# Delta-net layer: a pair's scales on VectorE, longer waits in the key chain, the last gate group ahead of the values, the gate sums with the decays

## The chip, the cores and the metric

The kernel runs on one core of a Trainium2 chip. The metric is the time of one execution on the device in microseconds; the runs shown are three of the kernel before. A profile of one execution shows what TensorE (PE, with its weight loads PEld), VectorE (DVE), ScalarE (ACT), GpSimd (POOL) and the DMA queue of SyncE (SP) did.

## The reference

The program is a two-layer trunk over 256 tokens of 1024 features in float32. Each layer has three parts, each between two RMS norms and added to the running state h: a SwiGLU block, a mixer, and a second SwiGLU block. Layer 0's mixer is a gated short convolution. Layer 1's mixer, the one that the change touches, is a gated delta-net:

- a projection gives queries and keys (8 heads of 128 features), values and output gates z (16 heads of 128), and two small columns per value head, b and a;
- q, k and v pass a causal convolution of width 4 and a silu; q and k are normalized to unit length;
- beta = sigmoid(b), and g = -exp(a_log) softplus(a + dt_bias) is a log decay per token and head;
- per head a state S follows S_t = a_t S_{t-1} (I - b_t k_t k_t^T) + b_t k_t v_t^T, o_t = S_t^T q_t, in chunked form: within a chunk a lower triangular matrix of decayed, beta-scaled key products is inverted;
- o is RMS-normalized, multiplied by silu(z), and projected back to 1024 features.

## The kernel before

Tokens are two tiles of 128 (t = 0, 1). Every float32 product is made from three TensorE products: a weight is split into a rounded part hi (ScalarE copy, L111) and the rest lo (VectorE subtraction, L113), and so is the activation. A weight unit is 128 x 1024: its DMA goes into one of 3 raw buffers, and hi and lo take one of 8 buffers each. Seven parts follow one another on PE: SwiGLU, mixer and SwiGLU of each layer, with an out-projection after each; in all but the delta-net they are dense matmuls with little between them.

The delta-net part (`gdn_proj`, about 668 to 930 us of the span) is a main line of dense matmuls, between which chains of small dependent steps are laid:

- The main line: the head slabs (b, a and the first seven key and query tiles, with the activation stationary), then nine more key and query tiles (`stat_group`, L248 to L250, weights stationary, 24 matmuls of 256 columns a tile), then the gate groups z 0, 1, 2 (`z_group`: `act_group`, L216 to L220, 48 matmuls of 512 columns a group, and a silu into a gate tile), then the value groups 0 to 3 (`v_group`, 96 matmuls of 256 columns each), then z group 3, then the out-projection (`out_proj`, L293 to L295, six matmuls a step).
- The ticker: after every 6 matmuls of `act_group`, every 12 of `stat_group` and every step of the out-projection, `tk.tick()` lets each chain advance to its next `yield`. `yield n` means: go on n ticks later. So the ticks set in what place of the program a chain's instructions stand. A planner then orders each engine's queue when the program is built: it takes that place as the priority and may put an instruction earlier when, by its own estimate, those ahead of it are not ready.
- `gates()` (L472) turns b and a into beta and the log decays g, and sums g over tokens by two small matmuls (L498, L499) with two exponentials behind them (L500, L501: `etail`, `eg`). It runs when the first head slab of t = 1 is done. `decays()` (L503) builds for four groups of four heads the products `gu` (L512), waits for the first convolved key (`while not convs`), and makes the decay matrices (L520 matmul, L522 exponential, L523 mask on GpSimd).
- `kq_raw` convolves a key or query tile (L548 on ScalarE, three steps L550 on VectorE) and takes its silu (L537).
- `kq_chain` (L569) goes through the 8 key heads in 4 pairs. A head waits until KQ_WAIT = 3 ticks after its silu; then come four transposes (L582), the key products (L585), and on ScalarE the copies and sums of squares (L594). Then the pair's scales: epsilon added to the sums (L598, GpSimd), reciprocal (L600, VectorE), times beta (L603, twice, GpSimd). VectorE scales and masks the products (L609, 8 instructions) and ScalarE copies the 32x32 diagonal blocks out (L616, 8). GpSimd makes three more small values (L618 a power, L620, L622). `yield 1` ends a pair. All heads and pairs take their PSUM from the same four banks.
- `invert()` (L631) starts when the chain has ended: VectorE transposes the blocks and inverts them in 62 dependent steps (L641, L643), and INV_WAIT = 37 ticks after its start the matmuls that build the full inverses begin (L671 to L703).
- `v_pair` convolves a pair of value tiles, and V_WAIT = 4 ticks later transposes them (L721). `scan(gi)` waits for its values and its inverse, then goes through solve (L735), intra-chunk product (L744), state (L775, L784) for t = 0, then solve and product for t = 1. `z_chain(gi, t)` waits for the scan's output scale, multiplies it into the gate tile (L810), transposes (L815) and splits it (L818, L819) into the operand of the out-projection.
- The out-projection takes its operands through `view.get`, which ticks on by itself until the one it wants exists. While `tail[0]` is false, the chains' PSUM banks (`side_bank`) come from the pool that the out-projection accumulates in; afterwards from the main line's pool.

Gate tiles, values, solutions and scan outputs share 22 slab slots; the scaled products take 8 larger ones.

Of the kernel before, what the change touches and what calls it, by code (L numbers as in the profile page):

```python
# [21 lines left out]
NG = 4  # L22
B32 = 32
EPS = 1e-6
# [6 lines left out]
NSMALL = 22  # L31
NBIG = 8
NROW = 3
KQ_WAIT = 3
INV_WAIT = 37
V_WAIT = 4
SCAN_WAIT = 2
# [13 lines left out]
def trunk_kernel(ctx: ExitStack, tc: tile.TileContext, x, norm_g, w_gu, w_dn, sc_in, sc_cw, sc_out,  # L51
# [389 lines left out]
    def gdn_proj(xh, xl, mid):  # L441
# [25 lines left out]
        def side_bank():  # L467
            return (ps if tail[0] else ps_acc).tile([P, 4, P], F32, name="mm" if tail[0] else "acc")
# [3 lines left out]
        def gates():  # L472
            def sm(name):
                return sp.tile([P, NT, NVH], F32, name=name, bufs=1)

            a, u, e, z, q = sm("ga"), sm("gb"), sm("gc"), sm("gd"), sm("ge")
            G.tensor_tensor(a, ba[:, :, NVH:], bc(dtb, NT), ALU.add)
            G.tensor_scalar(u, a, 0.0, -2.0, ALU.max, ALU.mult)
            G.tensor_tensor(e, a, u, ALU.add)
            S.activation(e, e, AF.Exp)  # L480
            S.activation(al, al, AF.Exp)
            S.activation(beta, ba[:, :, 0:NVH], AF.Exp, scale=-1.0)

            V.tensor_scalar(z, e, 2.0, None, ALU.add)
            V.reciprocal(z, z)
            V.tensor_tensor(z, z, e, ALU.mult)
            V.tensor_tensor(u, z, z, ALU.mult)
            V.tensor_scalar(q, u, 1.0 / 19.0, None, ALU.mult)
            for k in (17, 15, 13, 11, 9, 7, 5, 3):
                V.scalar_tensor_tensor(q, q, 1.0 / k, u, ALU.add, ALU.mult)  # L490
            V.scalar_tensor_tensor(q, q, 1.0, z, ALU.add, ALU.mult)
            V.tensor_scalar(a, a, 0.0, None, ALU.max)
            V.scalar_tensor_tensor(q, q, 2.0, a, ALU.mult, ALU.add)
            V.scalar_tensor_tensor(g, q, -1.0, bc(al, NT), ALU.mult, ALU.mult)
            G.tensor_scalar(beta, beta, 1.0, None, ALU.add)
            V.reciprocal(beta, beta)
            pg = side_bank().rearrange("p a b -> p (a b)")[:, 0:2 * NVH].rearrange("p (t n) -> p t n", t=NT)
            PE.matmul(pg[:, 0, :], lhsT=tri_s, rhs=g[:, 0, :], start=True, stop=True)  # L498
            PE.matmul(pg[:, 1, :], lhsT=tri_u, rhs=g[:, 1, :], start=True, stop=True)  # L499
            S.activation(etail, pg[:, 0, :], AF.Exp)  # L500
            S.activation(eg, pg[:, 1, :], AF.Exp)  # L501

        def decays():  # L503
            gus = []
            for gi in range(NG):
                gu = big([P, NT, 4, P], F32, "gu")
                for t in range(NT):
                    if 2 * gi + t < GUACT:
                        for hv in range(4):
                            S.activation(gu[:, t, hv, :], tri_u, AF.Copy, scale=g[:, t, 4 * gi + hv:4 * gi + hv + 1])  # L510
                        continue
                    V.tensor_tensor(gu[:, t], bc(tri_u, 4),  # L512
                                    g[:, t, 4 * gi:4 * gi + 4].unsqueeze(2).broadcast_to([P, 4, P]), ALU.mult)
                gus.append(gu)
            while not convs:
                yield 1
            for gi in range(NG):
                for t in range(NT):
                    pd = side_bank()
                    PE.matmul(pd, lhsT=tri_s, rhs=gus[gi][:, t], start=True, stop=True)  # L520
                    d = slab([P, 4, P], F32, "dec")
                    last_exp[0] = S.activation(d, pd, AF.Exp).ins  # L522
                    G.affine_select(d, d, pattern=[[0, 4], [1, P]], compare_op=ALU.is_ge, fill=0.0, base=0,  # L523
                                    channel_multiplier=-1)
                    dec[t][gi] = d
                if gi % 2:
                    yield 1
            dec_done[0] = True
            while convs:
                kq_silu(*convs.pop(0))  # L530
# [38 lines left out]
        def kq_chain():  # L569

            for gi in range(NG):
                ss = sp.tile([P, NT, 2, 2], F32, name="kss", bufs=2)
                k1 = slab([P, 2, 2, P], F32, "kq1")
                pkq = []
                for i in range(2):
                    kh = 2 * gi + i
                    while kq[kh] is None or tk.now < kq_time[kh] + KQ_WAIT:
                        yield 1
                    tp = side_bank().rearrange("p (t c) d -> p t c d", t=NT)
                    for t in range(NT):  # L580
                        for c in range(2):
                            PE.transpose(tp[:, t, c, :], kq[kh][:, c, t * P:(t + 1) * P], ident)  # L582
                    pk = side_bank().rearrange("p (t c) d -> p t c d", t=NT)
                    for t in range(NT):
                        PE.matmul(pk[:, t, :, :], lhsT=kq[kh][:, 0, t * P:(t + 1) * P],  # L585
                                  rhs=kq[kh][:, :, t * P:(t + 1) * P], start=True, stop=True)
                    pkq.append(pk)
                    S.activation(ktok[:, kh, :], tp[:, 0, 0, :], AF.Copy)
                    S.activation(k1[:, i, :, :], kq[kh][:, :, P:], AF.Copy)
                    kq1[kh] = k1[:, i, :, :]  # L590
                    for t in range(NT):
                        for c in range(2):
                            junk = sp.tile([P, 512], mybir.dt.bfloat16, name="junk", bufs=1)
                            S.activation(junk[:, 0:P], tp[:, t, c, :], AF.Square, accum_out=ss[:, t, c, i:i + 1])  # L594
                    yield 1
                while dec[1][gi] is None:
                    yield 1
                G.tensor_scalar(ss, ss, EPS, None, ALU.add)  # L598
                rk = sp.tile([P, NT, 2], F32, name="rk", bufs=2)
                V.reciprocal(rk, ss[:, :, 0, :])  # L600
                dd = small(f"dsc{gi}", 8).rearrange("p (t n) -> p t n", t=NT)
                for t in range(NT):
                    G.tensor_tensor(dd[:, t, :].rearrange("p (k v) -> p k v", k=2),  # L603
                                    beta[:, t, 4 * gi:4 * gi + 4].rearrange("p (k v) -> p k v", k=2),
                                    rk[:, t, :].unsqueeze(2).broadcast_to([P, 2, 2]), ALU.mult)
                for t in range(NT):
                    m = big([P, 4, 2, P], F32, "KQ")
                    for hv in range(4):
                        V.scalar_tensor_tensor(m[:, hv, :, :], pkq[hv // 2][:, t, :, :], dd[:, t, hv:hv + 1],  # L609
                                               bc(dec[t][gi][:, hv, :], 2), ALU.mult, ALU.mult)  # L610
                    KQ[gi][t] = m
                    for b in range(4):
                        r = slice(b * B32, (b + 1) * B32)
                        o = Ld[r, :, 8 * gi + t:8 * gi + t + 7:2].rearrange("p i v -> p v i")
                        i_ = m[r, :, 0, b * B32:(b + 1) * B32]
                        S.activation(o, i_, AF.Copy)  # L616
                n = small(f"nk{gi}", 4).rearrange("p (t n) -> p t n", t=NT)
                G.tensor_tensor(n, ss[:, :, 0, :], phalf.rearrange("p (t n) -> p t n", t=NT), ALU.pow)  # L618
                q = small(f"eq{gi}", 4).rearrange("p (t n) -> p t n", t=NT)
                G.tensor_scalar(q, ss[:, :, 1, :], 128.0 * EPS, None, ALU.mult)  # L620
                w = small(f"wt{gi}", 4)
                G.tensor_tensor(w, etail[:, 4 * gi:4 * gi + 4], dd[:, 0, :], ALU.mult)  # L622
                Dsc[gi], nk[gi], eq[gi], wt[gi] = dd, n, q, w
                yield 1
            tk.start(invert())


# [194 lines left out]
        def z_group(gi):  # L822
            w = load_slab(gdn_z[gi])
            for t in range(NT):
                pt = ps.tile([P, 512], F32, name="mm")
                act_group(pt, w, t, xh, xl)
                zs = slab([P, 4, P], F32, "zs")
                silu(zs, pt.rearrange("p (h d) -> p h d", h=4))
                tk.start(z_chain(gi, t, zs))
# [48 lines left out]
                    stat_group(pt[:, j, :], w, (2 * i + j) * P, xh, xl)  # L878
                tk.start(v_pair(gi, i, pt, tiles))

        for gi in range(NG - 1):
            z_group(gi)
        for gi in range(NG):
            v_group(gi)
        z_group(NG - 1)
        tail[0] = True

        def view(hs):
# [115 lines left out]
```

## Time and profile before

| | |
|---|---|
| runs | 1131.45, 1131.49, 1133.35 us; median 1131.49 |
| profiled execution | 1134.7 us, of which the span from first to last instruction 1132.9 |
| mean granted TensorE clock | 0.994 |
| busy | PE 1096.3 us (97%), PEld 941.8 (83%), DVE 748.1 (66%), ACT 652.3 (58%), POOL 88.7 (8%) |
| share of the chain that ended last | PE 75%, DVE 8%, ACT 6%, DMA 5%, issue 3%, POOL 2% |

PE's busy time is modelled for matmuls that overlap, so 97% busy is not the peak rate; but idle time on PE is real. A wait of an engine is shown with what released it. The granted clock is 1.00 at 2.4 GHz and 0.50 at 1.2 GHz.

### The profile page before, as it was taken

How to read it: one execution, taken by the hardware profiler on the slowest of the kernel's cores; microseconds unless marked ns; L12 is line 12 of the kernel's file. 1: busy time of each engine (PE TensorE's matmuls, PEld its weight loads, DVE VectorE, ACT ScalarE, POOL GpSimd, SP SyncE). 2: the span in 40 equal slices, each digit the busy share in tenths (PEclk: the TensorE clock that was granted, in tenths of full speed). 3: DMA queues.
4: the chain of work that ended last, by engine and by line, in shares of the span. 5: the costliest groups of instructions: out<-in, count | busy, mean ns of one | idle time of the engine just before them, and what ended most of it. 6: DMA issues, size and time to landing. Idle time of an engine off the chain costs nothing.

```text
span 1132.9 us, 16811 instructions
## 1 busy us (share of the span) xinstructions
PE 1096.3 (97%) x6272; PEld 941.8 (83%) x6272; DVE 748.1 (66%) x1137; ACT 652.3 (58%) x1203; POOL 88.7 (8%) x165
## 2 busy tenths in 40 slices
PE   6999999999999999999999999889899999999997
PEld 5888887788788888788888877868899887888886
DVE  5677735687777673577765478768956657767543
ACT  5665634545556663556664458784587645666432
POOL 2000000000110000010000012110051212000000
PEclk9999999999999999999999999999899999999999
DMA  7766555666565555577554653237342354665552
GB/s 255 236 195 207 176 177 176 207 186 199 186 209 196 194 186 170 165 225 214 184 195 167 189 185 115 85 102 223 113 132 76 120 165 173 213 204 181 191 167 75
DMA packets 55953, 198.64 MB, mean 175 GB/s; under 512 B 6720, under 2 KB 7232, under 8 KB 55872
## 3 DMA queue, kind: packets, MB, share of 16 engines
q1 hardware_dynamic: 55872, 197.58, 53.8%
q8 instruction: 49, 0.80, 0.3%
q14 instruction: 32, 0.26, 0.1%
HBM read 196.51 MB, written 1.05 MB: 174 GB/s over the span
## 4 chain that ended last, share of the span: by engine, by line
PE 75%; DVE 8%; ACT 6%; DMA 5%; issue 3%; POOL 2%; SPq 0%; DVEq 0%; POOLq 0%; ACTq 0%
PE mm L268 24%; PE mm L271 12%; PE acc L294 7%; PE acc L295 7%; PE acc L293 7%; PE mm L216 3%; PE mm L217 3%; PE mm L220 3%; DVE wlo L113 3%; DMA raw<-in_sc_in 2%; ACT whi L111 2%; ACT blk L616 1%; DVE kq L550 1%; ACT junk L145 1%; PE mm L171 1%
## 5 line engine op out<-in xcount | busy, mean ns | idle before, releaser
L113 DVE TENSOR_TENSOR wlo<-raw,whi 128x1024 fp32r<-128x1024 f32 (+2 forms) x362 | 437.9, 1220 | 243.0 <-ACT whi L111 208.3
L111 ACT ACTIVATE whi<-raw 128x1024 fp32r<-128x1024 f32 (+2 forms) x362 | 376.4, 1052 | 234.7 <-PE acc L295 104.2
L268 PE MATMUL mm<-x,whi 128*128 128x512 f32 x1312 | 329.4, 393 | 0.0
L268 PEld LDWEIGHTS mm<-x,whi 128*128 128x128 f32 x1312 | 235.9, 189 | 42.2
L271 PEld LDWEIGHTS mm<-x,wlo 128*128 128x128 f32 x1312 | 179.0, 190 | 12.8
L271 PE MATMUL mm<-x,wlo 128*128 128x256 f32 x1312 | 182.9, 282 | 0.0
L293 PE MATMUL acc<-whi,hb 128*128 128x512 f32 x352 | 136.6, 388 | 0.7 <-ACT hb L437 0.7
L294 PE MATMUL acc<-wlo,hb 128*128 128x512 f32 x352 | 135.7, 385 | 0.3 <-DVE wlo L113 0.3
L295 PE MATMUL acc<-whi,hb 128*128 128x512 f32 x352 | 135.5, 385 | 0.0
L217 PE MATMUL mm<-wlo,x 128*128 128x512 f32 (+1 forms) x240 | 95.0, 396 | 1.9 <-DVE wlo L113 1.9
L216 PE MATMUL mm<-whi,x 128*128 128x512 f32 (+1 forms) x240 | 95.4, 398 | 0.8 <-ACT x L173 0.7
L278 ACT ACTIVATE corr<-mm 128x256 f32<-128x256 f32 x164 | 60.6, 375 | 60.4 <-PE mm L271 59.9
L220 PE MATMUL mm<-whi,x 128*128 128x512 f32 (+1 forms) x240 | 88.8, 392 | 0.0
L293 PEld LDWEIGHTS acc<-whi,hb 128*128 128x128 f32 x352 | 66.2, 188 | 14.1 <-ACT hb L437 1.1
L294 PEld LDWEIGHTS acc<-wlo,hb 128*128 128x128 f32 x352 | 66.2, 188 | 13.8 <-DVE wlo L113 0.8
L295 PEld LDWEIGHTS acc<-whi,hb 128*128 128x128 f32 x352 | 66.1, 188 | 13.6 <-DVE hb L438 0.4
L151 POOL TENSOR_SCALAR rstd<-ss 128x1 f32<-128x1 f32 x24 | 12.2, 509 | 821.1 <-ACT junk L145 821.1
L248 PE MATMUL mm<-x,whi 128*128 128x256 f32 x200 | 60.3, 302 | 2.0 <-DVE kq L550 2.0
L249 PE MATMUL mm<-x,whi 128*128 128x256 f32 x200 | 59.0, 295 | 0.0
L250 PE MATMUL mm<-x,wlo 128*128 128x256 f32 x200 | 58.5, 292 | 0.0
L217 PEld LDWEIGHTS mm<-wlo,x 128*128 128x128 f32 x240 | 45.7, 191 | 12.4 <-DVE wlo L113 4.0
L216 PEld LDWEIGHTS mm<-whi,x 128*128 128x128 f32 x240 | 45.7, 191 | 10.9 <-ACT x L173 2.4
(208 smaller groups left out, 1231.1 us busy)
## 6 DMA issues: line engine op xcount, KB each, us to landing
raw<-in_w_gu SPq DMA_DIRECT2D x176, 512.0 KB, 4.1
raw<-in_w_dn SPq DMA_DIRECT2D x88, 512.0 KB, 3.6
raw<-in_sc_in SPq DMA_DIRECT2D x24, 512.0 KB, 4.0
raw<-in_gdn_z SPq DMA_DIRECT2D x16, 512.0 KB, 3.8
raw<-in_gdn_v SPq DMA_DIRECT2D x16, 512.0 KB, 4.2
raw<-in_gdn_out SPq DMA_DIRECT2D x16, 512.0 KB, 3.7
gamma<-in_norm_g SPq DMA_DIRECT2D x12, 512.0 KB, 5.6
raw<-in_gdn_a SPq DMA_DIRECT2D x9, 512.0 KB, 4.2
```

What stands on the lines that cost most here:

```text
L111: S.activation(hi[:, r], raw[:, r], AF.Copy)
L113: V.tensor_tensor(lo[:, r], raw[:, r], hi[:, r], ALU.subtract)
L216: PE.matmul(pt, lhsT=xh[:, t, k, :], rhs=hi, start=(k == 0), stop=False)
L217: PE.matmul(pt, lhsT=xh[:, t, k, :], rhs=lo, start=False, stop=False)
L220: PE.matmul(pt, lhsT=xl[:, t, j, :], rhs=part(j)[0], start=False, stop=(j == KD - 1))
L248: PE.matmul(ptile, lhsT=hi, rhs=h2, start=(k == 0), stop=False)
L268: PE.matmul(flat, lhsT=part(k, 0), rhs=xx[:, k].rearrange("p h t q -> p (h t q)"), start=(k == 0), stop=False)
L271: PE.matmul(flat[:, T:], lhsT=part(k, 1), rhs=xx[:, k, 0].rearrange("p t q -> p (t q)"), start=False, stop=(k == KD - 1))
L278: S.activation(c, pt[:, 1, :], AF.Copy)
L293: PE.matmul(o, lhsT=yh(c, t), rhs=hi[:, r], start=(c == 0), stop=False)
L294: PE.matmul(o, lhsT=yh(c, t), rhs=lo[:, r], start=False, stop=False)
L295: i = PE.matmul(o, lhsT=yl(c, t), rhs=hi[:, r], start=False, stop=(c == n - 1)).ins
```

## The change

Four edits, all in `gdn_proj`:

1. The epsilon add and the two products with beta of each pair move from GpSimd to VectorE.
2. KQ_WAIT becomes 5, and a pair of the key chain ends with `yield PAIR_WAIT` (3) where it was `yield 1`.
3. All four z groups come ahead of the value groups; before, the fourth came behind them.
4. The sums of the log decays, with their exponentials, leave `gates()` for a function of their own, `gate_sums()`, which `decays()` calls when the first convolved key is there.

```diff
@@ -31,7 +31,8 @@
 NSMALL = 22
 NBIG = 8
 NROW = 3
-KQ_WAIT = 3
+KQ_WAIT = 5
+PAIR_WAIT = 3
 INV_WAIT = 37
 V_WAIT = 4
 SCAN_WAIT = 2
@@ -494,6 +495,8 @@
             V.scalar_tensor_tensor(g, q, -1.0, bc(al, NT), ALU.mult, ALU.mult)
             G.tensor_scalar(beta, beta, 1.0, None, ALU.add)
             V.reciprocal(beta, beta)
+
+        def gate_sums():
             pg = side_bank().rearrange("p a b -> p (a b)")[:, 0:2 * NVH].rearrange("p (t n) -> p t n", t=NT)
             PE.matmul(pg[:, 0, :], lhsT=tri_s, rhs=g[:, 0, :], start=True, stop=True)
             PE.matmul(pg[:, 1, :], lhsT=tri_u, rhs=g[:, 1, :], start=True, stop=True)
@@ -514,6 +517,7 @@
                 gus.append(gu)
             while not convs:
                 yield 1
+            gate_sums()
             for gi in range(NG):
                 for t in range(NT):
                     pd = side_bank()
@@ -595,12 +599,12 @@
                     yield 1
                 while dec[1][gi] is None:
                     yield 1
-                G.tensor_scalar(ss, ss, EPS, None, ALU.add)
+                V.tensor_scalar(ss, ss, EPS, None, ALU.add)
                 rk = sp.tile([P, NT, 2], F32, name="rk", bufs=2)
                 V.reciprocal(rk, ss[:, :, 0, :])
                 dd = small(f"dsc{gi}", 8).rearrange("p (t n) -> p t n", t=NT)
                 for t in range(NT):
-                    G.tensor_tensor(dd[:, t, :].rearrange("p (k v) -> p k v", k=2),
+                    V.tensor_tensor(dd[:, t, :].rearrange("p (k v) -> p k v", k=2),
                                     beta[:, t, 4 * gi:4 * gi + 4].rearrange("p (k v) -> p k v", k=2),
                                     rk[:, t, :].unsqueeze(2).broadcast_to([P, 2, 2]), ALU.mult)
                 for t in range(NT):
@@ -621,7 +625,7 @@
                 w = small(f"wt{gi}", 4)
                 G.tensor_tensor(w, etail[:, 4 * gi:4 * gi + 4], dd[:, 0, :], ALU.mult)
                 Dsc[gi], nk[gi], eq[gi], wt[gi] = dd, n, q, w
-                yield 1
+                yield PAIR_WAIT
             tk.start(invert())
 
 
@@ -878,11 +882,10 @@
                     stat_group(pt[:, j, :], w, (2 * i + j) * P, xh, xl)
                 tk.start(v_pair(gi, i, pt, tiles))
 
-        for gi in range(NG - 1):
+        for gi in range(NG):
             z_group(gi)
         for gi in range(NG):
             v_group(gi)
-        z_group(NG - 1)
         tail[0] = True
 
         def view(hs):
```

## Rows read from the trace of the kernel before

**Rows 1.** The page's 40 slices of the span (28.3 us each): PE's busy tenths
```profile
PE   6999999999999999999999999889899999999997
```

**Rows 2.** PE's waits, 660 to 920 us: line, releaser, total us, times, longest
```profile
PE mm L721 <- ACT yb L537: 4.0, 1, 4.0
PE acc L582 <- ACT kq L537: 3.6, 2, 3.1
PE mm L248 <- DVE kq L550: 2.0, 1, 2.0
...
PE acc L585 <- DVE KQ L609: 1.7, 1, 1.7
PE acc L582 <- ACT junk L594: 1.1, 2, 0.7
PE acc L498 <- DVE glog L494: 1.0, 1, 1.0
```

**Rows 3.** Busy time by windows: window, length, PE, PEld, DVE, ACT, POOL, PEclk, DMA
```profile
732.00:752.00 20.00, 14.35 (x87) 12.09 (x86) 15.84 (x33) 18.35 (x58) 4.08 (x12) 1.00 0.22 59
763.00:818.00 55.00, 49.72 (x321) 45.92 (x319) 49.70 (x102) 28.57 (x40) 0.00 (x0) 0.94 0.56 170
```

**Rows 4.** The same view around the resumption after the longest wait
```profile
798.00:806.00 8.00, 6.21 (x32) 6.22 (x33) 7.98 (x20) 5.08 (x8) 0.00 (x0) 0.57 0.36 93
```

**Rows 5.** PE's timeline: start, us, engine, line, operation, tiles, [idle before it]
```profile
751.83 0.66 PE L582 MATMUL acc<-ident,kq 128*128 128x128 f32 x4 [3.06 <-ACT kq L537]
752.33 1.03 PE L585 MATMUL acc<-kq 128*128 128x256 f32 x4
...
818.31 0.38 PE L671 MATMUL acc<-blk,KQ 32*32 32x32 f32 x12 [0.22 <-DVE blk L645]
...
844.91 0.36 PE L248 MATMUL mm<-x,whi 128*128 128x256 f32 x1
...
847.86 0.61 PE L744 MATMUL acc<-ysol,KQ 128*128 128x128 f32 x4
...
862.44 0.40 PE L216 MATMUL mm<-whi,x 128*128 128x512 f32 x1
...
863.83 1.95 PE L735 MATMUL acc<-rsol,KQ 128*128 128x128 f32 x16
...
870.60 2.84 PE L744 MATMUL acc<-ysol,KQ 128*128 128x128 f32 x24
...
884.54 1.03 PE L815 MATMUL mm<-ident,zs 128*128 128x128 f32 x8
```

**Rows 6.** Windows of L216 alone (first row) and of L248 alone (two rows)
```profile
738.00:762.69 24.69, 8.02 (x21) 4.12 (x22) 1.00 0.30 94
...
782.50:799.70 17.20, 10.18 (x36) 6.86 (x36) 0.96 0.56 178
782.50:818.31 35.81, 22.74 (x76) 15.62 (x76) 0.90 0.51 151
```

**Rows 7.** Chain that ended last, 695 to 713 us: start, us, what
```profile
697.45 4.21 DVE gu L512 x7
701.67 9.77 DVE kq L550 x18
```

**Rows 8.** GpSimd's timeline at the last pair
```profile
754.34 0.24 POOL L598 TENSOR_SCALAR kss<-kss 128x8 f32<-128x8 f32 x1 [11.96 <-ACT junk L594]
754.66 1.04 POOL L618 TENSOR_TENSOR nk<-kss,phalf 128x4 f32<-128x4 f32 x1
...
756.08 0.35 POOL L603 TENSOR_TENSOR dsc<-beta,rk 128x4 f32<-128x4 f32 x2
```

**Rows 9.** VectorE's timeline at the last pair
```profile
754.61 0.18 DVE L600 RECIPROCAL rk<-kss 128x4 f32<-128x4 f32 x1 [1.96 <-POOL kss L598]
756.32 3.23 DVE L609 SCALAR_TENSOR_TENSOR KQ<-acc,dsc,dec 128x256 f32<-128x256 f32 x8 [1.53 <-POOL dsc L603]
...
762.69 1.25 DVE L633 STREAM_TRANSPOSE blk<-blk 128x1024 f32<-128x1024 f32 x1 [2.01 <-ACT blk L616]
```

## The prediction, made before the changed kernel was run

> **What bounds the kernel now.** I read the slices of the page first. PE is at 9 tenths nearly everywhere; past the start and before the end, 8s stand only in slices 26, 27 and 29, that is 708 to 765 and 793 to 821 us, in the delta-net projection [rows 1]. Elsewhere PE has nothing to give, and the change adds or removes no TensorE work. So only PE's idle time in the delta-net, and its low clock there, can be won or lost. The list of PE's waits from 660 to 920 us names that idle time [rows 2]:
>
> - the key chain: transposes L582 wait 3.6 us for the silu of a head and 1.1 for the sums of squares L594, products L585 wait 1.7 for the scaling L609: 6.4 us together;
> - the first value transposes L721: one wait of 4.0 us;
> - the gate sums L498: 1.0; the bank of a conv (L248 on L550): 2.0.
>
> The windows then say which engine is short. From 732 to 752 ScalarE is busy 18.35 of 20 us while PE does 14.35; from 763 to 818, while VectorE inverts the 32x32 blocks, VectorE is busy 49.70 of 55 [rows 3]. The 4.0 us wait has a second price: the window 798 to 806 shows a mean granted clock of 0.57, so some 6.9 us of it at 1.2 instead of 2.4 GHz (0.43 x 8 / 0.5), of which about 5 us after PE resumed at 799.79: 2.5 us of work lost [rows 4].
>
> The Trainium skill (TensorE: Matmul & The Clock Gate, HAM oscillation) says that idle gaps between groups of matmuls drop this clock. Here the trace agrees after the wait of 4.0 us, but the 3.1 us wait at 748.8 left the window 732 to 752 at 1.00 [rows 3]. By the rule alone that wait would hide another 2.5 us and the sum would be -9.7; I charge the clock only where a row shows it.
>
> **Counting ticks.** Chains advance on ticks. An activation-stationary step (gates z) ticks every 6 matmuls, 1.39 us (862.44 to 863.83); a weight-stationary one (keys, values) every 12, half of 844.91 to 847.86, 1.48 us [rows 5]. From the code, the key weights end at tick 34. Before: gates 0 to 2 are ticks 35 to 58, values 59 to 90, gate 3 91 to 98; pairs are scaled at 26, 29, 32 and 38, the inversion is issued at 40 and its matmuls L671 at 77. After, with a wait of 5 for a head and 3 behind a pair: all gates 35 to 66, values 67 to 98; pairs at 28, 33, 38, 43, inversion 47, L671 at 84. The trace confirms the count: 36 L248 of the value groups (4 a tick, so tick 67) precede the L721 that waits, and 76 (tick 77) precede L671 [rows 6].
>
> **Gate sums with the decays: 0.** PE no longer stops 1.0 us for the log gates. But VectorE runs without a hole through the decay products from 697.45 and 18 conv steps from 701.67, which end at 711.44 [rows 7], and PE waits for one of these convs until about 712. What PE saves is waited for there. The two exponentials that move along are first read by a pair's scales, at tick 28, nine ticks on. The ends are -1.0 (all kept) and +2.5 (the longer gap brings a second low-clock phase like that of [rows 4]).
>
> **Scales on VectorE.** Per pair GpSimd loses three instructions and VectorE gains three. Of the last pair: the epsilon add starts at 754.34, but the power for the norms (1.04 us) goes ahead of the two products, which begin at 756.08 [rows 8]; VectorE starts scaling at 756.32 [rows 9]. The trace has none of these operations on VectorE; the nearest is the reciprocal on 4 elements, 0.18 us [rows 9]. The add, the reciprocal and two products at 0.18 end 0.72 us after 754.34 instead of 1.98: 1.26 us earlier. Bounds: 2 us a pair (they overlap, nothing else delayed) to -0.7 (they hold up VectorE and GpSimd had been free). I take 1.26; queued behind them on VectorE are weight residues L113, which today stand behind the reciprocal's wait for GpSimd anyway.
>
> A rule speaks against it: the Trainium skill (VectorE: DVE Perf Modes, Rules for kernel authors) wants the count of VectorE operations kept down. By that, 12 more of 0.18 cost 2.2 us and the sum would be -5.0; by the rows nothing, because VectorE idles 1.96 and 1.53 us around this reciprocal [rows 9].
>
> **Longer waits: -4.5.** The last head's transposes move from tick 37 to 42, 5 gate ticks or 7 us of matmuls later; and when its silu is traced ScalarE has one pair and three heads less ahead of it. So the 3.1 us wait goes. With three ticks behind a pair, the 1.7 us for L609 and the 1.1 for L594 are covered by 2 x 1.4 to 1.5 us more matmuls and the 1.26 us. ScalarE stays the tightest engine, so I leave 1.9 of the 6.4 standing. Ends: -6.4 and 0.
>
> **Gate group 3 ahead of the values: -5.5.** Today VectorE starts the inversion at 762.69 [rows 9], when PE has done 21 L216 of the gates (2 a tick: tick 44.5 [rows 6]): 4.5 ticks after it was issued. That lag is what L721 waits for, since its conv is queued on VectorE among the inversion's steps. After: from the last L582 (751.83 before [rows 5]) to the inversion are 10.86 us, now 9.6; less 1.5 of PE's own key products (751.83 to 753.36) that is 8.1 us or 5.8 ticks past tick 42: tick 47.8, under one tick late. L721 is due at 75 instead of 67, the same distance from the inversion's issue, and the lag it paid for is gone: 4.0 + 2.5 = 6.5 us. What is late next is L671: from 47.8 to 84 PE has 18.2 gate ticks x 1.39 + 18 value ticks x 1.48 + three sets of four transposes of 0.5 (as 751.83 to 752.33 [rows 5]) = 53.4 us, while the inversion took 55.4 (762.69 to its last L645, 0.22 us after which L671 starts at 818.31 [rows 5]). If it is as long again PE waits 2.0 us; it is shorter where PE's own lateness held it up (convs that wait for value products). I keep 1.0. Ends: -6.5 and 0. The group's four weight DMAs go ahead of sixteen value DMAs on SP, in the order in which PE now wants both; its four splits (ScalarE, VectorE) and two silus move with them. Its two gate tiles are held some 30 ticks longer: by the code at most 20 to 22 of the 22 slab slots are then taken, so I charge nothing; with none free, a solve L735 would wait for a tile to be read, 1 to 2 us.
>
> **Its price at the end: +2.8.** Gate 3 used to stand between the scans and the out-projection. By count the first transposed output exists at tick 100, while the out-projection's first step would come at 99, so two ticks pass with no dense matmuls: 2 x 1.39. The scans' own products fill part (L735, L744: 2.84 us at 870.60 [rows 5]); end 0. Later needs (second half at c=6, groups 2 and 3 at c=8 and 12) have one tick of slack where they had six or seven. Other end: rival B.
>
> **Sum.** -4.5 - 5.5 + 2.8 = -7.2. The profiled execution took 1134.7 us (span 1132.9, 1.8 outside), 3.2 above the median of the runs; it becomes 1127.5, and the median 1131.49 becomes **1124.3** (own range 1119 to 1129).
>
> **Rivals.**
> A: ScalarE sets the key chain, and the inversion starts 3 to 4 us late. For: 18.35 of 20 busy [rows 3]. Against: its block copies wait for VectorE's scalings, which now come 1.26 us earlier in a pair. Then L721 or L671 waits that much again: 1127.5 to 1131, say 1129.3.
> B, slower: the out-projection needs the scans before anything covers them. Between L744's end, 873.44, and the next output transposes at 884.54 lie 11.1 us [rows 5], filled today by five gate ticks and one out step (8.3 us). If the out steps that should fill them wait for their own weights, since eight weight buffers still hold the values' units and ScalarE and VectorE convert the new ones behind the scans' squares, 8.3 us lie bare, with 2.8 ahead and one clock fall (2.5): 13.6 against gains of 10.0. 1135.1. It decides from 10 us of idle PE between L744 and the sixth out step. Against: PE has no wait there now [rows 2].
> C: the waits do not do what they say. Queue order is fixed by a planner that may pull work ahead (the power stands ahead of the products [rows 8], behind them in the code). Key-chain waits of 6.4 stay, only the last pair's 1.3 counts: -1.3 - 5.5 + 2.8, 1127.5.
>
> **Chances.** Forecast 0.50, A 0.24, B 0.16, C 0.10. About 0.2% (2.3 us) is what a measurement tells from none: faster is below 1129.2, slower above 1133.8. Faster: 0.47 + 0.12 + 0.08 = 0.67; same: 0.03 + 0.10 + 0.04 + 0.02 = 0.19; slower: 0.02 + 0.12 = 0.14. Range 1118.5 to 1133.5, for both ends of the two gains and most of A.
>
> **What would show it.** Right: no L721 wait and clock 1.00 at that point; L582 and L585 waits under 2 us in total; the inversion's first transpose within a tick of its issue; out-projection waits under 4 us. Wrong: L671 or L721 waiting over 3 us (A), L293 waiting for L818 or weights by 8 us or more and a low clock near 870 (B), the key waits unchanged (C).

## The result, and the profile of the changed kernel

The changed kernel takes 1140.82 us (median of four, 1140.17 to 1141.79) against 1132.12 for the one before beside it: a ratio of 1.0075, 95% interval 1.0061 to 1.0088. It is 8.7 us slower where 7.2 faster was forecast. Five of the versions tried below (e4, e7, e8, e12, e17) take 9 to 20 us longer in some executions than in others, at a lower granted clock (e17: 0.979 against 0.992); the ratios leave out the most disturbed executions. The profiled execution took 1140.17 us (span 1138.5). In the changed kernel every line of the delta-net stands up to 4 further down: L582 is L586, L671 is L675, L696 is L700, L721 is L725.

The 40 slices of its page (28.5 us each), with the granted clock in tenths, answer to [rows 1]:

```profile
PE   6999999999999999999999998999789999999997
PEclk9999999999999999999999999999879999999999
```

The 8s of the key chain (slices 26 and 27) are gone; the 8 in slice 25 holds the waits for the log gates and for the bank of a conv (1.0 and 2.2 us), which were there before (1.0 and 2.0). The dip now fills slices 29 and 30, 797 to 854 us, is deeper, and the clock dips with it. PE's waits from 660 to 920 us, to lay beside [rows 2] (same columns; "acc L700" is the first product of 64x64 blocks of the inverse, and E and KQ are the tiles that these blocks are put together in):

```profile
PE mm L725 <- ACT yb L541: 7.5, 2, 6.4
PE acc L700 <- POOL E L668: 4.8, 1, 4.8
PE mm L249 <- DVE kq L554: 2.2, 1, 2.2
PE mm L218 <- DVE wlo L114: 1.4, 1, 1.4
PE acc L501 <- DVE glog L495: 1.0, 1, 1.0
```

All 6.4 us of the key chain have gone; the wait at the value transposes, which was to vanish, has grown from 4.0 to 7.5; and there is a new one of 4.8 us at L700, for GpSimd. The windows (columns as in [rows 3]) show what the two did to the clock; the first row answers to [rows 4]:

```profile
798.00:806.00 8.00, 1.64 (x8) 1.65 (x9) 7.86 (x22) 4.65 (x8) 0.00 (x0) 0.67 0.19 63
804.00:810.00 6.00, 5.64 (x36) 5.65 (x37) 6.00 (x17) 4.23 (x8) 0.00 (x0) 0.70 0.44 119
832.00:846.00 14.00, 13.78 (x147) 12.91 (x148) 2.89 (x6) 4.52 (x11) 3.42 (x10) 0.50 0.01 2
```

From 832 to 846 PE is busy 13.78 of 14 us and every microsecond of it is at 1.2 GHz. If the same work takes half of that at 2.4 GHz, 7 us are lost behind a wait of 4.8 (an estimate; e9 below measures 6.6). GpSimd's timeline says what it waited for:

```profile
815.91 15.05 POOL L657 COPY KQ<-blk 32x128 f32<-32x128 f32 x32 [53.31 <-DVE blk L651]
831.00 0.83 POOL L667 COPY E<-blk 32x256 f32<-32x256 f32 x2
831.87 0.30 POOL L668 MEMSET E<- 32x256 f32 x1
```

The same view of before:

```profile
818.32 1.72 POOL L663 COPY E<-blk 32x256 f32<-32x256 f32 x4 [60.43 <-DVE blk L645]
...
821.68 12.47 POOL L653 COPY KQ<-blk 32x128 f32<-32x128 f32 x32
```

Before, the first E copies, which L696 reads, stood ahead of the 32 diagonal copies; in the changed kernel they stand behind them. No line of this code was edited. In the code the diagonal copies (L657) come first, and the E copies (L667) follow INV_WAIT = 37 ticks behind them: it was the planner that had put the first E copies ahead in the kernel before, and in the changed kernel it did not.

ScalarE's and VectorE's timelines at the last pair answer to [rows 8, 9], and the third fence is the window of L217 alone up to the inversion's start, to lay beside [rows 6]:

```profile
758.63 0.19 ACT L598 ACTIVATION_READ_ACCUMULATOR junk<-acc 128x1 f32 x1
...
762.73 1.84 ACT L620 ACTIVATE blk<-KQ 32x128 f32<-32x128 f32 x4 [0.96 <-DVE KQ L613]
...
765.56 1.80 ACT L620 ACTIVATE blk<-KQ 32x128 f32<-32x128 f32 x4
```
```profile
759.35 0.17 DVE L602 TENSOR_SCALAR kss<-kss 128x8 f32<-128x8 f32 x1
759.54 0.18 DVE L604 RECIPROCAL rk<-kss 128x4 f32<-128x4 f32 x1
759.76 0.23 DVE L607 TENSOR_TENSOR dsc<-beta,rk 128x4 f32<-128x4 f32 x2
759.91 1.22 DVE L114 TENSOR_TENSOR wlo<-raw,whi 128x1024 fp32r<-128x1024 f32 x1
761.04 3.22 DVE L613 SCALAR_TENSOR_TENSOR KQ<-acc,dsc,dec 128x256 f32<-128x256 f32 x8
...
767.39 1.25 DVE L637 STREAM_TRANSPOSE blk<-blk 128x1024 f32<-128x1024 f32 x1 [2.00 <-ACT blk L620]
```
```profile
730.00:767.39 37.39, 15.79 (x39) 7.34 (x39) 1.00 0.38 119
```

PE's last key transposes in the changed kernel, and the end of the sums of squares in the kernel before:

```profile
750.86 0.60 PE L586 MATMUL acc<-ident,kq 128*128 128x128 f32 x4
```
```profile
754.06 0.19 ACT L594 ACTIVATION_READ_ACCUMULATOR junk<-acc 128x1 f32 x1
```

The scales themselves cost what was forecast. But ScalarE ends the last sums of squares at 758.8, 8.0 us after PE's last L586 began (750.86); before, that was 2.4 us (754.25 against 751.83). So the inversion starts when PE has done 39 L217 of the gates, tick 53.5: 6.5 ticks after it is issued, where the forecast had 0.8. From the last squares to the inversion it is 8.6 us (8.4 before), so on this last pair the scales on VectorE saved nothing: a weight residue (759.91) went in between, and L613 starts 2.2 us after the squares, as before (2.1).

### The profile page after: what moved, and what is told of

Its sections match the earlier page's. It is cut to its first block, busy times and chain, and to the rows that moved or that the text cites. A ratio compares the mean times of both kernels' runs of the same rounds, so it can differ in the third digit from the quotient of the medians.

```text
span 1138.5 us, 16812 instructions
## 1 busy us (share of the span) xinstructions
PE 1100.4 (97%) x6272; PEld 946.5 (83%) x6272; DVE 751.2 (66%) x1149; ACT 654.3 (57%) x1203; POOL 84.9 (7%) x153
## 4 chain that ended last, share of the span: by engine, by line
PE 82%; DVE 6%; ACT 6%; DMA 3%; issue 2%; POOL 1%; SPq 0%; DVEq 0%; POOLq 0%; ACTq 0%
PE mm L269 27%; PE mm L272 14%; PE acc L295 8%; PE acc L294 8%; PE acc L296 8%; PE mm L217 3%; PE mm L218 3%; PE mm L221 3%; DVE wlo L114 2%; ACT whi L112 2%; PE mm L249 1%; ACT blk L620 1%; PE mm L251 1%; PE mm L250 1%; PE mm L172 1%
## 5 line engine op out<-in xcount | busy, mean ns | idle before, releaser
L217 PE MATMUL mm<-whi,x 128*128 128x512 f32 (+1 forms) x240 | 95.6, 398 | 0.8 <-ACT x L174 0.6
L218 PE MATMUL mm<-wlo,x 128*128 128x512 f32 (+1 forms) x240 | 94.4, 393 | 1.6 <-DVE wlo L114 1.6
L218 PEld LDWEIGHTS mm<-wlo,x 128*128 128x128 f32 x240 | 45.5, 190 | 12.3 <-DVE wlo L114 3.6
L217 PEld LDWEIGHTS mm<-whi,x 128*128 128x128 f32 x240 | 45.5, 190 | 11.1 <-ACT x L174 2.3
```

The lines of the kernel that those rows point to most:

```text
L217: PE.matmul(pt, lhsT=xh[:, t, k, :], rhs=hi, start=(k == 0), stop=False)
L218: PE.matmul(pt, lhsT=xh[:, t, k, :], rhs=lo, start=False, stop=False)
```

## The experiments

Theory Q: the loss is GpSimd's order (wait and clock) and the late inversion. Rivals: Z, the move of group 3 costs by itself; K, the longer waits cost by delaying the inversion; P, the wait comes back at the next small product. Medians are over 4 to 12 executions, beside before at 1131.9 to 1133.2; behind each stands the ratio to before with its 95% interval. Line numbers are each version's own. The diffs show the lines that matter, with their indentation taken off; "..." marks a cut.

**What makes GpSimd's order, and what it costs**

e6, before with that order alone:

```diff
-G.tensor_copy(KQ[gi][t][r, :, 0, r], Yd[r, 8 * gi + t:8 * gi + t + 7:2, :])
+kqc = G.tensor_copy(KQ[gi][t][r, :, 0, r], Yd[r, 8 * gi + t:8 * gi + t + 7:2, :]).ins
...
-G.tensor_copy(E[gi][r, :, r], Xd[r, 8 * gi:8 * gi + 8, :])
+with tc.issue_after(kqc):
+    G.tensor_copy(E[gi][r, :, r], Xd[r, 8 * gi:8 * gi + 8, :])
...
-G.memset(E[gi][0:B32, :, B32:], 0.0)
+with tc.issue_after(kqc):
+    G.memset(E[gi][0:B32, :, B32:], 0.0)
```

> Before, with the E copies and memsets held behind the 32 diagonal copies on GpSimd: the order that the changed kernel has, and nothing else. Theory Q: before's E copies are there at 820.4 and its L696 starts at 824.6; with 13.2 us of diagonal copies from 818.3 ahead of them they come at 832.4, so L696 waits some 7.8 us, and the clock falls to 0.50 behind it for 6 to 12 us: 1140 to 1146 us. Rival P (PE finds other work, or the order does nothing): 1131 to 1133 us.

Measured 1145.39 us, ratio 1.0106 (1.0092 to 1.0120). PE's longest wait (L698 is before's L696):

```profile
PE acc L698 <- POOL E L666: 9.9, 1, 9.9
```

The order alone makes the kernel before 13.3 us slower: TensorE's and VectorE's instructions stand in the same order in both traces. e10, the same diff in edits 1, 3 and 4 (e2 below):

> Edits 1, 3 and 4 without 2 (1128.3 us), with the E copies held behind the diagonal copies on GpSimd, as in after. Theory Q: with the inverse at hand at 813.5, 13.2 us of diagonal copies put the E copies at 827.5 to 829.5, and L699, at 818.8 in the version without this, waits 8 to 10 us; with the clock behind it 1138 to 1146 us, as slow as after: then the queue order alone is what separates after from the version without longer waits. Rival K (the longer waits cost by starting the inversion late, the order is a side effect): under 1132 us.

Measured 1151.06 (ratio 1.0156, 1.0138 to 1.0174): 22.8 us above the version without it, more than either theory said; K's "under 1132" falls. The wait was 8.3 us as forecast, and behind it the clock stood at 0.50 for a whole window:

```profile
826.00:850.00 24.00, 23.80 (x288) 21.69 (x289) 6.33 (x9) 11.55 (x25) 3.38 (x10) 0.50 0.22 67
```

To take the order out of the changed kernel took three tries. e1 issues the first half's E copies early:

```diff
+for gi in (0, 1):
+    E0[gi] = slab([P, 8, 64], F32, "E64")
+    for b in range(2):
+        r = slice(b * B32, (b + 1) * B32)
+        G.tensor_copy(E0[gi][r, :, r], Xd[r, 8 * gi:8 * gi + 8, :])
+    G.memset(E0[gi][0:B32, :, B32:], 0.0)
 for gi in range(NG):
     for t in range(NT):
...
```

> After, with the first half's E copies and their memset issued ahead of the 32 diagonal copies KQ<-blk on GpSimd (nothing else in the code is changed). Theory Q (the loss of the changed kernel sits in two places: GpSimd's queue, where the 32 diagonal copies of 15 us now stand before the E copies that L700's bank waits for, 4.8 us, and the low clock of 832 to 846 that follows, 5 to 6 us; and the late start of the inversion, which L725 pays with 7.5 us): the wait at L700 is under 0.5 us, the granted clock from 830 to 846 is above 0.9, and the time is 1130 to 1133 us, 8 to 10 below after. Rival Z (the move of gate group 3 costs by itself, because values, scans and out-projection now follow one another with nothing between, so that a wait removed in one link comes back in the next): the wait at L700 goes but solves, products or the out-projection wait as much; 1138 to 1142 us.

Measured 1145.17 (1.0113, 1.0099 to 1.0127). L700's wait went, but the planner moved L675 (L684 here) into the middle of gate group 3 (8 of its 16 L217 come behind it), where PE stood for the inverse:

```profile
PE acc L684 <- DVE blk L649: 23.0, 1, 23.0
```

So it told nothing of the order's price. e5 is e1 with L675 held behind the value matmul that it follows in the changed kernel:

```diff
-PE.matmul(ptile, lhsT=lo, rhs=h2, start=False, stop=(k == KD - 1))
+last_pe[0] = PE.matmul(ptile, lhsT=lo, rhs=h2, start=False, stop=(k == KD - 1)).ins
...
-PE.matmul(pt[r1, x, :], lhsT=m[r0, (ht // 2) % 4, 0, r1], rhs=Xd[r0, ht, :],
-          start=True, stop=True)
+with tc.issue_after(last_pe[0]):
+    PE.matmul(pt[r1, x, :], lhsT=m[r0, (ht // 2) % 4, 0, r1], rhs=Xd[r0, ht, :],
+              start=True, stop=True)
```

> After, with the first half's E copies ahead of the 32 diagonal copies on GpSimd, and with the first products of the inverse (L675) held behind the value matmul that they follow in after (S 400 of the value groups' matmuls), since in the run before this one they had moved ahead of the last gate group and PE stood 23 us there. Theory Q: L725's wait of some 6 us stays, L700 waits under 0.5 us instead of 4.8, the clock from 826 to 846 is above 0.9: 1129 to 1133 us. Rival P (the second low clock belongs to the small products themselves and the wait of 4.8 us comes back at the next small product that needs a diagonal copy, L707): 1137 to 1141 us.

Measured 1139.14 (1.0055, 1.0041 to 1.0069). L700's wait is gone again, and 5.3 us at L218 (L217 of the changed kernel) for the silu of a gate tile (L542) are new, with 8.3 at the value transposes. The time is in P's range, but not by P's wait (the changed kernel's L707 waits for nothing here); another one took the place, so it is inconclusive. e9 gives the E tiles buffers of their own; TensorE's order in the delta-net stays as it was:

```diff
-NSMALL = 22
+NSMALL = 20
...
-E[gi] = slab([P, 8, 64], F32, "E64")
+E[gi] = hp.tile([P, 8, 64], F32, name="E64", tag="E64", bufs=2)
```

> After with two buffers of their own for the E tiles (and 20 instead of 22 for the other slabs): the E copies then stand ahead of the 32 diagonal copies on GpSimd, with TensorE's and VectorE's order in the delta-net as in after (a few layer-0 instructions change places). Theory Q: L725 waits some 7 us as in after, L700 under 0.5 us instead of 4.8, and the clock from 826 to 846 stays above 0.9: 1129 to 1133 us. Rival P (the wait comes back at the next small product, or the clock falls all the same): 1137 to 1141 us.

Measured 1129.68 (0.9970, 0.9955 to 0.9985), 11.1 us below the changed kernel. The E copies come first, L700 doesn't wait, and the same small products run at 2.4 GHz:

```profile
PE mm L725 <- ACT yb L541: 7.2, 2, 6.2
```
```profile
826.00:846.00 20.00, 20.00 (x442) 18.67 (x442) 5.57 (x9) 15.74 (x41) 7.36 (x21) 0.99 0.15 53
```

P falls. PE's instructions stand in the same order in both kernels here, so the price can be read off: its first L686 starts at 824.3 in the changed kernel and 825.3 in e9, its last L707 at 856.6 and 846.2. That is 11.4 us lost between, of which 4.8 are the wait at L700 and 6.6 the clock. That the E tiles' place in the shared slabs makes the order is shown by this (their own buffers and the 20 slots are not told apart); why the planner hands them their slab so late is not.

**Which edit brings it**

e2, without edit 2:

```diff
-KQ_WAIT = 5
+KQ_WAIT = 3
...
-yield PAIR_WAIT
+yield 1
```

> After without edit 2 (KQ_WAIT 3 and one tick behind a pair, as before). Theory Q: the key chain's 6.4 us of waits are there again, but the inversion is issued at tick 40, so L725 (tick 75) no longer waits; the E copies stand ahead of the diagonal copies on GpSimd, so L700 doesn't wait for them; L675 (tick 77) may wait 0 to 5 us. 1126 to 1132 us, at or below before. Rival Z: as slow as after or slower by the key waits, 1138 to 1146 us. Rival K (the longer waits are a gain that is only hidden): 1146 us.

Measured 1128.27 (0.9967, 0.9955 to 0.9979): faster than before, with the E copies first. The key chain waits 2.8 us, not 6.4: edits 1, 3 and 4 take more than half of it. The first value transposes wait 3.2. Z falls here as the account of the loss, and so does K's price (1146). With e9 it prices edit 2: 0.9967 without the longer waits, 0.9970 with them, both with the E copies first. So the longer waits gained nothing in time (e9's own buffers are the one other difference): the key chain's 2.8 us go with them, but L725 waits 7.2 us in e9 against 3.2 here. e7, half of edit 2:

```diff
-PAIR_WAIT = 3
+PAIR_WAIT = 1
```

> After with one tick behind a pair (PAIR_WAIT 1) and KQ_WAIT 5 kept: half of edit 2. The inversion is then issued at tick 44 instead of 47; in this build the E copies stand ahead of the diagonal copies on GpSimd. Theory Q: L725's wait falls from 7.5 to 2 to 4 us, L700's goes, the key waits stay near 0 to 2: 1126 to 1131 us. Rival K (the longer wait for a head is what delays the inversion): 1136 to 1142 us.

Measured 1131.65 (1.0006, 0.9987 to 1.0025; 1129.3 to 1140.8): the E copies come first. Its profile is of an execution of 1139.46 us; there L725 waits 4.7 us and L589 3.3, both more than Q had. Its median is a little above Q's range and below K's. e12, edit 3 alone, in before:

```diff
-for gi in range(NG - 1):
+for gi in range(NG):
     z_group(gi)
...
-z_group(NG - 1)
```

> Before with edit 3 alone (gate group 3 ahead of the values). In this build the diagonal copies stand ahead of the E copies on GpSimd, and L671 behind 132 value matmuls (tick 78). Theory Q: L721's wait of 4.0 us goes, but L671 waits 2 to 5 us and the bank of L696 or its E copies 3 us or more, with the clock behind them: 1134 to 1144 us. Rival M (the move is a gain by itself, as the prediction had it at -5.5): 1125 to 1129 us.

Measured 1141.92 (1.0072, 1.0054 to 1.0090), no execution under 1139.71. M falls. e3, the changed kernel with that diff taken back:

> After without edit 3 (gate group 3 behind the values, as before, with the longer waits). Theory Q: the key waits are gone (-6.4), but the inversion starts some 9 ticks later than before while L725 stays at tick 67, and the diagonal copies stand ahead of the E copies: L725 waits 8 us or more, L675 or L700 5 us or more, 1138 to 1148 us. Rival Z (the move of group 3 is what costs): 1125 to 1128 us.

Measured 1140.94 (1.0076, 1.0063 to 1.0089), with 7.3 us at L700 and 6.7 at L725: within Q's range, and Z falls. Longer waits without the move, and the move without longer waits and scales, each put the diagonal copies first (traces of e3 and e12).

**What the move of group 3 is worth with the order held.** e14 is e12, and e13 is e3, each with e9's diff.

> Before with the move of group 3 alone, with the E tiles in two buffers of their own (with the shared slabs 1141.9 us, 8.0 us at L721 and 3.4 at L696). Theory Q: L696's wait goes, L721's stays at 6 to 8 us, since the planner lets its conv stand behind the inversion's steps: 1131 to 1137 us, no gain. Rival M: 1126 to 1128 us, the move is worth its 5.5 us.

Measured 1136.80 (1.0044, 1.0028 to 1.0061), 4.2 us above before beside it; L721 waits 6.8 us where before waits 4.0. Before with own E buffers and no move was not run, so what the buffers do to before by themselves is not shown.

> Edits 1, 2 and 4 without the move of group 3, with the E tiles in two buffers of their own, so that the E copies stand ahead of the diagonal copies on GpSimd (with the shared slabs this version took 1140.9 us, with 7.3 us at L700 and 6.7 at L725). Theory Q: L700's wait goes, L725's stays at 6 to 7 us: 1129 to 1133 us, so the move of group 3 is worth 0 to 3 us in this company, as L725 waits as long with it. Rival M (the move is worth the forecast's 5.5 us): 1135 us, 5.5 above the mended changed kernel.

Measured 1128.36 (0.9967, 0.9955 to 0.9978), against 1129.68 with the move (e9; 0.9970): nothing gained, as Q said.

**Who makes the inversion late.** e16 is e9 with ScalarE relieved:

```diff
-S.activation(o, i_, AF.Copy)
+G.tensor_copy(o, i_)
```

> The changed kernel with E tiles in buffers of their own (1129.7 us), with the 8 diagonal block copies L620 of each pair on GpSimd instead of ScalarE, which has 3.6 us a pair less to do. Theory A (ScalarE sets the last pair: its sums of squares end 8 us behind PE's last transposes, 758.8 against 750.9, where before had 2.5): the sums of squares of the last pair end 3 us or more earlier, the inversion starts at 763 to 764 instead of 766.5, L725 waits 4 us or less: 1124 to 1127 us. Rival W (VectorE's weight residues, or weights that come late from memory, set it): the inversion starts within 1 us of 766.5, 1128 to 1132 us.

Measured 1123.65 (0.9926, 0.9910 to 0.9942; six executions within 0.6 us). ScalarE, VectorE and the waits, in three views:

```profile
751.72 0.20 ACT L598 ACTIVATION_READ_ACCUMULATOR junk<-acc 128x1 f32 x1
```
```profile
761.78 1.25 DVE L637 STREAM_TRANSPOSE blk<-blk 128x1024 f32<-128x1024 f32 x1 [2.16 <-POOL blk L620]
...
793.59 0.38 DVE L645 TENSOR_TENSOR sg<-blk 128x207 f32<-128x207 f32 x1
793.88 0.48 DVE L554 SCALAR_TENSOR_TENSOR yb<-mm,gcw,yb 128x255 f32<-128x255 f32 x1
```
```profile
PE mm L725 <- ACT yb L541: 4.2, 2, 3.1
```

The last squares end 3.4 us behind PE's last L586 (748.56) instead of 8.0; the inversion starts 4.8 us earlier than in e9 (766.54), of which 1.4 are PE's own (its last L586 came at 750.00 there), and the longest wait halves, more than A said. Theory A holds and W falls. On GpSimd the last pair's eight copies took 4.76 us, against 3.64 on ScalarE in the changed kernel: slower, and still the better place. The Trainium skill (GPSIMD Engine Reference, Engine selection) lists one-input work on GpSimd as roughly line rate, set against VectorE; no run here has these copies on VectorE. e18, the same with e12's diff taken back:

> The version of 1123.65 us (E tiles in buffers of their own, block copies on GpSimd) without the move of gate group 3. Theory L (the move is worth the forecast's 5.5 us only where the inversion starts about when it is issued): L725, 8 ticks nearer to the inversion's start, waits 4 to 7 us instead of 3.1 and the clock may fall: 1127 to 1130 us. Rival N (the move is worth nothing in any company, since the conv's place among the inversion's steps moves with it): 1122 to 1125 us.

Measured 1123.11 (0.9923, 0.9905 to 0.9942). L fell, N held: the move is worth nothing here either (0.9926 with it, 0.9923 without). The conv that L725 waits for shows why. Its place in e16 is in the fence above (the step ahead of it at 793.59); VectorE in e18:

```profile
782.76 0.43 DVE L645 TENSOR_TENSOR sg<-blk 128x255 f32<-128x255 f32 x1
783.10 0.48 DVE L554 SCALAR_TENSOR_TENSOR yb<-mm,gcw,yb 128x255 f32<-128x255 f32 x1
```

A step of 207 elements is the inversion's 23rd (9 x 23), one of 255 its 15th (17 x 15). With the move PE comes to L725 8 ticks later, and its conv stands 8 steps later in VectorE's queue, 10.8 us later (793.88 against 783.10).

**Walking around the wait by ticks.** Five tries with the constants alone; each is this diff with other numbers:

```diff
-INV_WAIT = 37
-V_WAIT = 4
+INV_WAIT = 39
+V_WAIT = 8
```

e4, the changed kernel with V_WAIT 8:

> After with V_WAIT 8 where it was 4: a value pair is transposed 8 ticks behind its conv. In this build the E copies also stand ahead of the diagonal copies on GpSimd again. Theory Q: PE meets its first L725 at tick 79, 4 ticks or 5.9 us later, so the wait there falls from 7.5 to under 2 us, the wait at L700 goes and the clock holds: 1124 to 1129 us. Rival Z: the later values make the scans late, solves L739 or the out-projection wait 5 us or more: 1136 to 1142 us.

Measured 1136.20 (1.0020, 1.0003 to 1.0037; 1129.5 to 1138.4). L725's wait falls to 0.6 us, L700's goes, and 5.7 us appear at L686, whose ScalarE copy (L679) stands behind a conv and a weight split: neither theory's place. The median is in Z's range; two executions of twelve (1129.5) come near Q's. e8, e2 with V_WAIT 6:

> Edits 1, 3 and 4 without 2 (1128.3 us) with V_WAIT 6: PE meets the first value transposes 2 ticks, 3 us, later. Theory Q: their wait of 3.2 us goes and nothing takes its place but up to 1.5 us at L674: 1124 to 1127 us. Rival W (the inversion's end is the limit, PE arrives at L674 3 us earlier and waits there instead): 1127.5 to 1130 us.

Measured 1126.58 to 1146.86 (1.0000, 0.9971 to 1.0029): L674 waits 4.7 us instead, as W said, but eight of the twelve executions lie above W's 1130. e11, with INV_WAIT 40 as well:

> Edits 1, 3 and 4 without 2, V_WAIT 6, and INV_WAIT 40 where it was 37: value transposes 2 ticks later and the products of the inverse 3 ticks later. With V_WAIT 6 alone L674 waited 4.7 us in a profile of 1126.6, and the same queues gave up to 1147 in other executions, at a lower clock. Theory Q with the clock (it is the wait before the small products that brings the clock down, in some executions and not in others): with L674 3 ticks, 4.4 us, later that wait is under 1 us, the clock stays above 0.995 and the time is 1122 to 1126 us in every execution. Rival T (the scans come too late for the out-projection): solves or the out-projection wait 3 us or more, 1127 to 1135 us.

Measured 1129.32 (0.9969, 0.9953 to 0.9985), and L674 still waits 4.7 us: a miss for both: the time is in T's range, but nothing waits for the scans. e15, e9 with V_WAIT 8 and INV_WAIT 39:

> The changed kernel with E tiles in buffers of their own (1129.7 us), V_WAIT 8 and INV_WAIT 39: value transposes 4 ticks, the products of the inverse 2 ticks later. Theory Q: L725's wait of 7.2 us falls under 1.5, L675 waits under 1.5 us, the clock from 798 to 850 stays above 0.97: 1120 to 1124 us. Rival T (what is put off comes back behind: scans too late for the out-projection, waits of 3 us or more there): 1125 to 1131 us.

Measured 1134.43 (1.0019, 1.0006 to 1.0032): the wait came back behind as 2.5, 2.2, 1.8 and 1.7 us: T's mechanism in smaller pieces, and dearer than T's 1131. e17, e16 with V_WAIT 6:

> The last version (E tiles in buffers of their own, block copies on GpSimd, 1123.65 us) with V_WAIT 6. Theory Q: the first value transposes come 2 ticks, 3 us, later and their wait of 3.1 us falls under 0.5; L675, which had 2.6 us between the inverse's end (811.5) and its own start (814.1), waits under 1 us: 1120 to 1122 us. Rival T (as with V_WAIT 8 and INV_WAIT 39, what is put off comes back behind, in L249, products or solves): 1123 to 1128 us.

Measured 1127.45 to 1143.61 (1.0062, 1.0030 to 1.0094): the first L725 no longer waits, a later one waits 4.9 us (profile of 1129.83). Q falls; T has the mechanism, but only two of twelve executions are in its range.

## Why the prediction was wrong, by its steps

- **Gate sums with the decays: 0.** Nothing speaks against the size, but no run takes edit 4 by itself. The reason was half wrong: PE still waits 1.0 us for the log gates.
- **Scales on VectorE.** Right in their cost: 0.17 us for the add, 0.18 for the reciprocal and 0.23 for both products, against 0.18 each. The 1.26 us gained is missing where the next step counts on it: on the last pair a weight residue of 1.22 us slipped in ahead of L613, and L613 started 2.2 us after the squares, as before.
- **Longer waits: -4.5.** The key waits went, all 6.4 us of them; but 3.6 of these go with edits 1, 3 and 4 alone (e2), and in time the longer waits gained nothing (0.9970 with, 0.9967 without). What the step left out is that ScalarE came to stand 8.0 us behind PE there, which L725 pays for.
- **Gate group 3 ahead of the values: -5.5.** This step failed, in two places. First, "4.0 + 2.5 = 6.5 us" came from counting ticks between the inversion's issue and L721. The wait is not set by that distance: the conv's place among the inversion's steps moves along with L721 (8 steps for 8 ticks), and what is left to wait for is how late VectorE's queue runs. Measured with the order held, the kernel is no faster with the move: 0.5 and 1.3 us slower by the medians (e16 against e18, e9 against e13), 0.0003 by both pairs of ratios, which is within their intervals; alone it is 4.2 slower (e14). Second, the 0.8 ticks of lag became 6.5: the working took 9.6 us from the last L582 to the inversion; it was 16.5 (750.86 to 767.39). Of the 6.9 us between, 5.6 are ScalarE's squares (8.0 against 2.4) and 1.3 the scales' gain that did not come. That is rival A's mechanism, shown by e16; A had 3 to 4 us.
- **"What is late next is L671 ... I keep 1.0."** L675 did not wait. (The 55.4 us of the inversion took PE's idle 0.22 for the time since L645, which ends at 818.25; it is 55.6, and nothing hangs on it.) The step stopped there, and did not follow GpSimd from the inverse to L700, though its E copies and diagonal copies were in the trace. This term, left out of the sum, is the largest: 4.8 us of wait and 6.6 of clock by the traces of e9 and the changed kernel, 11.1 by their medians. The slab sentence ("I charge nothing") saw the shared slots and priced another user of them, a solve: it is the E tiles' turn among them that sets GpSimd's order (e9). Whether the slots were short is not shown.
- **Its price at the end: +2.8.** Nothing: PE has no wait from 883 to 928, so rival B did not happen. The key waits of rival C did go, so C did not happen; but its ground, that queue order is fixed by a planner, is what decided.

With what was measured the sum is -6.4 (key chain) + 3.5 (L725) + 4.8 (L700) + 7.0 - 0.7 (clock: 832 to 846, and 1.8 at 804 to 810 in place of 2.5): +8.2, against +5.6 in span and +8.7 in the medians; the 2.6 us that it has over the span are not accounted for.

On the clock, three waits and what the granted clock was behind them:

```profile
752.00:760.00 8.00, 8.00 (x38) 6.72 (x38) 4.51 (x11) 5.30 (x17) 3.26 (x9) 1.00 0.49 183
```
```profile
798.00:806.00 8.00, 2.66 (x13) 2.66 (x14) 7.93 (x24) 5.30 (x9) 0.00 (x0) 0.57 0.23 72
```
```profile
798.00:802.00 4.00, 3.25 (x16) 3.25 (x17) 4.00 (x10) 3.22 (x7) 0.00 (x0) 0.57 0.39 110
802.00:826.00 24.00, 22.38 (x334) 21.21 (x333) 19.62 (x33) 15.12 (x30) 14.79 (x37) 1.00 0.52 159
```

They are before (3.1 us at 748.8), e9 (6.2 at L725) and e16 (3.1 at L725). The clock fell behind L725 in both, for longer in e9; behind the same 3.1 us before it did not. The prediction's window, up to 752, showed only 0.2 us of what came behind that wait; the row here says that it was right not to charge it. The Trainium skill (TensorE: Matmul & The Clock Gate, HAM oscillation) has idle gaps between groups of matmuls bring the clock down. The traces agree behind L700's 4.8 us (0.50) and both L725, and the wait before shows that not every gap does it; the section does not say so of every gap, as the prediction's "by the rule alone" took it.

## What to carry to other kernels

Where a planner fixes queue orders, lay each engine's order after an edit beside the one before, the idle engines' too: here a change of ticks put 15 us of GpSimd copies ahead of 2 us that PE needed. Here a wait for a late engine was not won by moving the one who waits, since its supplier's place in the queue moved along (e18); it was won by taking work off the late engine (e16: eight copies a pair to idle GpSimd, 6.0 us below e9). A version of edits 1, 2 and 4 with own E buffers and those copies moved beats both kernels: 1123.11 us, the move of group 3 left out.

## What was not expected of the hardware

- How long the clock stays down does not follow from the length of the wait. Behind waits of PE of 4.7 to 4.9 us it was at 0.50 for 2 to 4 us (e8, from 812), 6 (e11, 812 to 818), 13 (e17, 818 to 831) and 16 (changed kernel, 832 to 848); in e7 it was at 0.50 from 817 to 836 behind a wait of 1.55 us that ended at 816.5. What chooses is not shown.
- The clock can stay at 1.2 GHz while PE is busy: 24 us in e10 (23.80 busy), 19 in e7 (19.00 busy), 14 in the changed kernel (13.78). In e9 the same small products ran at 0.99.
- The inversion's 62 steps and their transposes ended 35 us after the first transpose when PE stood still for 23 of them and only eight weight residues came between (e1, 766.98 to 802.1), against 46.5 in the changed kernel and 55.6 before: other work in VectorE's queue, and what it waits for, stretch it by up to 58%.
